# DeltaNet merges: triangular blocks joined in pairs and then in halves, as small float32 products in several column groups

## The chip, the cores and the metric

The kernel runs on one core of one Trainium2 chip. The metric is the device time of one execution in microseconds (us), lower being better. The engines of a core work side by side: TensorE (matmuls; in the profile PE, its weight loads PEld), VectorE (DVE), ScalarE (ACT), GpSimd (POOL) and SyncE (SP), which issues most DMAs.

## The reference

The network is a two-layer trunk over 512 positions with 1024 channels. Layer 0 mixes tokens by a gated DeltaNet, layer 1 by a convolution module; each layer then has a cross-attention into 256 memory positions and a squared-ReLU MLP. The change lies in the DeltaNet, whose core solves a unit lower triangular system for each head and each chunk of positions:

```python
lower = jnp.where(strict, jnp.einsum("bhnik,bhnjk->bhnij", k_beta, k) * decay, 0.0)
a_mat = jnp.eye(DN_CHUNK, dtype=q.dtype) + lower
rhs = jnp.concatenate([v * beta[..., None], k_beta * jnp.exp(g_cum)[..., None]], axis=-1)
sol = lax.linalg.triangular_solve(a_mat, rhs, left_side=True, lower=True, unit_diagonal=True)
...
def step(state, inp):
    qd, kd, uc, wc, ai, gl = inp
    v_new = uc - jnp.einsum("bhck,bhkv->bhcv", wc, state)
    o = jnp.einsum("bhck,bhkv->bhcv", qd, state) + jnp.einsum("bhcj,bhjv->bhcv", ai, v_new)
    state = state * jnp.exp(gl)[..., None, None] + jnp.einsum("bhck,bhcv->bhkv", kd, v_new)
    return state, o
```

The kernel uses chunks of 128 positions (four chunks, eight heads of 128 channels), which gives the same output, and inverts the 128x128 triangular matrix of each head and chunk instead of solving with it.

## The kernel before

**Stages and order.** `run` (in the kernel's main function) walks through a list `mains` of TensorE work, one entry being half of a projection of 128 output columns (12 matmuls with 512 moving columns, lines 292 to 294, tile `h`), or a unit of the memory's keys and values (tiles `K`, `V`). Beside each entry it issues "sides", that is, pieces of the DeltaNet with their position in the list and a rank. TensorE executes its queue in the order in which it is written, so the sides' matmuls stand between two entries' matmuls. Every large product is split into three of a faster float32 format (`wh`, `wl` are the two parts of a weight, made by ScalarE and VectorE; `xh`, `xl` those of the input); the small products of the DeltaNet are plain float32.

**The inverse.** For each head `k2` makes the matrix `bt` (128x512: four chunks side by side), a transposed triangular matrix. The four diagonal blocks of 32x32 of each matrix are inverted together for four heads on VectorE (`fs_in`, `fs_begin`, `fs_steps`, `fs_end`). The "merges" then build the 128x128 inverse from these blocks:

- `mg_pre` clears the result tile `u0` and the diagonal blocks of `bt` (on GpSimd).
- `mg_a` copies the inverted blocks onto the diagonal of `u0` and transposes it blockwise on VectorE into `x0`.
- `mg_w` (line 689) multiplies `bt` with `x0`, one product for each chunk with 128 stationary and 96 moving columns; ScalarE evicts it negated into `w` (line 691).
- `mg_y` (line 701) runs three times, the last time as `mg_end`: it multiplies `w` with the latest term `y`, with 96, 64 and 32 stationary and moving columns. ScalarE copies the next `y` (line 704), VectorE adds the product into `u0` (a helper's line, 71). The inverse is thus a sum of powers.

The recurrence over the chunks (`rec`) reads the finished tile as `U[h]`.

**Places.** Four heads (`gq` = 0 or 1) are merged together; the position is `MG[gq]` in the list, 36 and 68. Two heads take a step in the same slot, the other two one slot later, so that five slots hold the merges of a group. In the first group projections `h` stand between the slots, in the second units of `K`. PSUM tiles (`psum`, eight banks) and SBUF tiles (`slot`, 69 of them) rotate.

Of the kernel before, what the change touches and what calls it, by code (L numbers as in the profile page):

```python
# [10 lines left out]
AF = mybir.ActivationFunctionType  # L11
ALU = mybir.AluOpType
AX = mybir.AxisListType

P = 128
# [22 lines left out]
def tile_trunk(ctx, tc, xT, memT, x_d, mem_d, prm_d, adt_d, bdw_d, tap_d, fin_d, w_ab, w_kq, w_v, w_z, w_dno, w_pw1, w_pw2,  # L38
               w_q, w_k, w_vv, w_o, w_up, w_dn, yT):
    nc = tc.nc  # L40
    pe, act, dve, pool = nc.tensor, nc.scalar, nc.vector, nc.gpsimd
# [10 lines left out]
    def nm(s):  # L52
        cnt[0] += 1
        return f"{s}_{cnt[0]}"

    def slot(dt=F32, s="u", shape=(P, NT)):
        return up.tile(list(shape), dt, tag="u", name=nm(s))

    def psum(s="ps"):
        return psp.tile([P, NT], F32, tag="ps", name=nm(s))  # L60
# [9 lines left out]
    def tt(e, o, a, b, op):  # L70
        r = e.tensor_tensor(out=o, in0=a, in1=b, op=op)  # L71
        if e is pool:
            last_pool[:] = [r]
        return r
# [10 lines left out]
    def c4(t):  # L85
        return t.rearrange("p (c i) -> p c i", c=4)
# [112 lines left out]
    for kind, gq in DN_ORDER:  # L199
        for i in range(2):  # L200
            j = gq * 2 + i
# [228 lines left out]
    class DeltaNet:  # L430
# [233 lines left out]


        def mg_pre(self, h):
            u0, bt = slot(s="u0"), self.BT.pop(h)
            pool.memset(u0, 0.0)
            for b in range(4):
                bs = slice(32 * b, 32 * b + 32)  # L670
                pool.memset(c4(bt)[bs, :, bs], 0.0)
            self.M[h] = u0, bt

        def mg_a(self, h):
            (u0, bt), n = self.M[h], slice(h % 4 * 4, h % 4 * 4 + 4)
# [6 lines left out]

        def mg_w(self, h):
            u0, x0, bt = self.M[h]
            ps = psum("mg")
            for c in range(4):
                pe.matmul(c4(ps)[:, c, 0:96], bt[:, c * P:(c + 1) * P], c4(x0)[:, c, 0:96], start=True, stop=True)
            w = slot(s="w")  # L690
            self.w = act.activation(c4(w)[:, :, 0:96], c4(ps)[:, :, 0:96], AF.Copy, scale=-1.0)
            self.M[h] = u0, u0, w, 1

        def mg_y(self, h):
            u0, y, w, n = self.M[h]
            ps = psum("mg")
            r = 128 - 32 * n
            k = slice(0, 128 if n == 1 else r + 32)
            cs = slice(32 * n, 128)
            for c in range(4):  # L700
                pe.matmul(c4(ps)[0:r, c, cs], c4(w)[k, c, 0:r], c4(y)[k, c, cs], start=True, stop=True)
            if n < 3:
                y = slot(s="y")
                act.copy(c4(y)[0:r, :, 32 * n + 32:128], c4(ps)[0:r, :, 32 * n + 32:128])
            tt(dve, c4(u0)[0:r, :, cs], c4(u0)[0:r, :, cs], c4(ps)[0:r, :, cs], ALU.add)
            self.M[h] = u0, y, w, n + 1

        def mg_end(self, h):
            self.mg_y(h)
            self.U[h] = self.M.pop(h)[0]  # L710


        def ev_v(self, h):
            self.M["v", h] = self.conv_raw(self.ps.pop(("v", h)))
# [171 lines left out]
    def mem_gain(layer, half):  # L886
        gn = f"xa_mem{layer}"
        if half == 0:
            mem["xs"] = []
        for j in (2 * half, 2 * half + 1):  # L890
            if layer == 1:
                m = mem["m"][j].rearrange("p (k t) -> p k t", k=2)
                tt(dve, m, m, over_c(mem["rs"][:, 0:256], 2), ALU.mult)
            mh = slot(F32R, "mh")
            ml = slot(F32R, "ml")
            for i in range(2):
                ks = slice(i * 256, (i + 1) * 256)
                src = mem["m"][j][:, ks]
                g = pc(gn, 2 * j + i)
                act.activation(mh[:, ks], src, AF.Copy, scale=g)  # L900
                stt(ml[:, ks], src, g, mh[:, ks].bitcast(F32), ALU.mult, ALU.subtract)
                mem["xs"].append((mh[:, ks], ml[:, ks]))
# [393 lines left out]
    def taps(m):  # L1296

        TAPS[m] = []
        for i in range(9):
            t = slot(s="tap")  # L1300
            nc.sync.dma_start(out=t, in_=tap_d[m - NTAP, i])
            TAPS[m].append(t)
# [239 lines left out]
    for i in range(4):  # L1542
        s = slice(i * 256, (i + 1) * 256)
# [29 lines left out]
    D = DeltaNet(n0)  # L1573
    mains, S = [], Sides()
# [68 lines left out]
    for gq in range(2):  # L1643
        f0, nf = FS[gq]
        S.at(f0, 5, D.fs_begin, gq)
        for i in range(nf):
            S.at(f0 + i, 6, D.fs_steps, gq, i * 31 // nf, (i + 1) * 31 // nf)
        S.at(f0 + nf, 1, D.fs_end, gq)
        for h in range(4 * gq, 4 * gq + 4):
            S.at(f0 + nf, 1, D.mg_a, h)  # L1650
        S.at(f0 + 1, 7, D.norm_k, gq)
        S.at(f0 + nf + 2, 7, D.norm_q, gq)
        for i in range(4):
            h = 4 * gq + i
            S.at(f0 + nf - 4 + i, 5, D.mg_pre, h)
            for j, f in enumerate((D.mg_w, D.mg_y, D.mg_y, D.mg_end)):
                S.at(MG[gq] + j + i // 2, 1, f, h)
        for c in range(4):
            u = at["v", 4 * gq + 3] + V2[gq]
            if gq == 0:  # L1660
                S.at(u, 3, D.v2, gq, c)
            else:
                S.at(u, 3, D.v2, gq, c, (0, 1, 2))
                S.at(u + 1, 0, D.v2, gq, c, (3,))
        n = 0
        for c in range(4):
            for step in range(3):
                S.at(REC[gq] + n, 0, D.rec, gq, c, step)
                n += 1
            S.at(REC[gq] + n + (c < 3 if gq == 1 else -(c == 1)), 5, D.o_gate, gq, c)  # L1670
        S.at(ONORM[gq], 1, D.o_norm, gq)
# [33 lines left out]
    h = []  # L1705
# [13 lines left out]
    h = xattn(0, n1, h, n2)  # L1719
    n3 = Norm("cv_norm")  # L1720
    h, rest = mlp7(0, n2, h, n3, lambda: (mem_gain(1, 0), mem_gain(1, 1), taps(NTAP)))
    n4 = Norm("xa_norm1")
    h = conformer(n3, h, n4, rest)
    n5 = Norm("mlp_norm1")
    h = xattn(1, n4, h, n5)
# [30 lines left out]
MG = (36, 68)  # L1756
# [119 lines left out]
```

## Time and profile before

| | us |
|---|---|
| three runs, median | 1465.74 |
| lowest and highest | 1464.31 and 1465.99 |
| the profiled execution | 1464.05 |
| its span in the profile | 1462.3 |
| TensorE busy in the merges' products (256 matmuls) | 20.79 |

The times are those of whole executions; the profile is of one further execution, and what lies between its time and its span is 1.75 us before the first and behind the last recorded instruction. Matmuls overlap, so that "busy" of one is longer than the step to the next: the time from the start of one matmul to the start of the next is what a product costs. Tile names are those of the program without their numbers; `u` in the rows is `u0`, and the products of merges are called `mg`. A stationary operand of 96 rows and 64 columns is written `96*64`.

### The profile page before, as it was taken

What the parts mean: (1) busy time and instruction counts of PE and PEld (TensorE: products, weight loads), DVE (VectorE), ACT (ScalarE), POOL (GpSimd) and SP (SyncE); (2) the same over time, 40 slices, a digit from 0 to 9 for tenths busy, and PEclk for the clock granted to TensorE, in tenths of its full rate; (3) what the DMA queues carried; (4) which work ended last, traced back from release to release, by engine and by line L of the source; (5) the groups of instructions that cost most, each with busy time, mean ns of one, the idle gap of its engine ahead of it and who ended that gap; (6) DMA issues with size and microseconds to landing.
All of it is one profiled execution on the core that took longest, in us unless ns stands there. A gap on an engine that the chain in (4) does not pass through costs nothing.

```text
span 1462.3 us, 19656 instructions
## 1 busy us (share of the span) xinstructions
PE 1453.4 (99%) x7310; PEld 1226.7 (84%) x7310; DVE 1065.9 (73%) x1618; ACT 771.2 (53%) x1328; POOL 266.8 (18%) x289
## 2 busy tenths in 40 slices
PE   9999999999999999999999999999999999999998
PEld 7888889988888888888888889988888888888886
DVE  6879889867646766767679899985555766767677
ACT  7856865655434464435355655564444554434354
POOL 1411310103113000010000487402113000000100
PEclk9999999999999999999999999999999999999999
DMA  8232124442213666575766624533214566575853
GB/s 288 80 116 72 59 87 159 134 141 87 72 44 109 165 165 180 140 200 134 202 159 216 184 81 164 178 130 100 72 46 130 138 170 178 138 210 128 216 160 87
DMA packets 62880, 201.83 MB, mean 138 GB/s; under 512 B 7744, under 2 KB 10304, under 8 KB 62784
## 3 DMA queue, kind: packets, MB, share of 16 engines
q1 hardware_dynamic: 52560, 164.39, 33.4%
q0 software_dynamic: 9792, 35.66, 14.1%
q8 instruction: 57, 0.93, 0.3%
q10 hardware_dynamic: 432, 0.52, 0.1%
q14 instruction: 39, 0.32, 0.1%
HBM read 197.66 MB, written 2.10 MB: 137 GB/s over the span
## 4 chain that ended last, share of the span: by engine, by line
PE 93%; DVE 3%; ACT 2%; issue 1%; POOL 1%; DMA 1%; SPq 0%; DVEq 0%; POOLq 0%; ACTq 0%
PE up L294 8%; PE up L292 8%; PE up L293 8%; PE dn L1130 6%; PE dn L1128 6%; PE dn L1129 6%; PE pw L294 3%; PE pw L292 3%; PE pw L293 3%; PE h L292 2%; PE h L294 2%; PE h L293 2%; PE xo L293 2%; PE q L293 2%; PE q L292 2%; PE xo L292 2%
## 5 line engine op out<-in xcount | busy, mean ns | idle before, releaser
L251 ACT CAST wh<-raw 128x1024 fp32r<-128x1024 f32 x259 | 271.7, 1051 | 360.2 <-issue 97.0
L71 DVE TENSOR_TENSOR wl<-raw,wh 128x1024 fp32r<-128x1024 f32 (+1 forms) x250 | 304.3, 1219 | 105.7 <-ACT wh L251 99.6
L292 PE MATMUL up<-xh,wh 128*128 128x512 f32 x512 | 199.7, 390 | 0.0
L294 PE MATMUL up<-xh,wl 128*128 128x512 f32 x512 | 199.3, 389 | 0.0
L293 PE MATMUL up<-xl,wh 128*128 128x512 f32 x512 | 199.2, 389 | 0.0
L294 PEld LDWEIGHTS up<-xh,wl 128*128 128x128 f32 x512 | 96.1, 188 | 20.1
L293 PEld LDWEIGHTS up<-xl,wh 128*128 128x128 f32 x512 | 96.1, 188 | 19.9
L292 PEld LDWEIGHTS up<-xh,wh 128*128 128x128 f32 x512 | 96.1, 188 | 19.8
L239 POOL DMA_DIRECT2D t<-w_dn x48 | 42.2, 916 | 370.0 <-DVE wl L71 249.8
L1128 PE MATMUL dn<-wh,ah 128*128 128x512 f32 (+1 forms) x260 | 100.6, 387 | 0.0
L1130 PE MATMUL dn<-wl,ah 128*128 128x512 f32 (+1 forms) x260 | 100.4, 386 | 0.0
L1129 PE MATMUL dn<-wh,al 128*128 128x512 f32 (+1 forms) x260 | 100.4, 386 | 0.0
L77 DVE SCALAR_TENSOR_TENSOR rl<-up,rb 128x512 f32<-128x512 f32 x64 | 44.2, 690 | 58.3 <-PE up L294 58.3
L1388 DVE SCALAR_TENSOR_TENSOR ca<-x,prm,ca 128x512 f32<-128x512 f32 x112 | 82.3, 753 | 3.9 <-ACT ca L1385 1.5
L251 ACT CAST wh<-t 128x1024 fp32r<-128x1024 f32 x44 | 46.4, 1054 | 54.3 <-PE dn L1129 43.7
L71 DVE TENSOR_TENSOR wl<-t,wh 128x1024 fp32r<-128x1024 f32 x44 | 53.7, 1224 | 27.9 <-ACT wh L251 27.8
L292 PE MATMUL h<-xh,wh 128*128 128x512 f32 x184 | 73.7, 400 | 0.0
L71 POOL TENSOR_TENSOR sq<-sq,sq 128x512 f32<-128x512 f32 x28 | 45.4, 1620 | 148.3 <-ACT sq L385 134.2
L294 PE MATMUL h<-xh,wl 128*128 128x512 f32 x184 | 71.9, 391 | 0.0
L293 PE MATMUL h<-xl,wh 128*128 128x512 f32 x184 | 71.7, 390 | 0.0
L71 DVE TENSOR_TENSOR acc<-acc,dn 128x512 f32<-128x512 f32 x99 | 66.7, 683 | 1.2
L71 DVE TENSOR_TENSOR al<-u,ah 128x512 fp32r<-128x512 f32 x64 | 44.1, 689 | 21.4 <-ACT ah L331 21.4
(392 smaller groups left out, 3564.7 us busy)
## 6 DMA issues: line engine op xcount, KB each, us to landing
raw<-w_dn SPq DMA_DIRECT2D x68, 512.0 KB, 3.8
raw<-w_up SPq DMA_DIRECT2D x64, 512.0 KB, 4.5
t<-w_dn POOLq DMA_DIRECT2D x48, 512.0 KB, 5.8
raw<-w_pw SPq DMA_DIRECT2D x24, 512.0 KB, 3.7
raw<-w_dn POOLq DMA_DIRECT2D x20, 512.0 KB, 6.0
raw<-w_k SPq DMA_DIRECT2D x16, 512.0 KB, 3.6
raw<-w_vv SPq DMA_DIRECT2D x16, 512.0 KB, 3.9
t<-w_dn SPq DMA_DIRECT2D x16, 512.0 KB, 4.5
```

Of the source, the lines that this page charges most:

```text
L71: r = e.tensor_tensor(out=o, in0=a, in1=b, op=op)
L77: return dve.scalar_tensor_tensor(out=o, in0=a, scalar=s, in1=b, op0=op0, op1=op1)
L239: nc.gpsimd.dma_start(out=t, in_=a, accum_op=ALU.add)
L251: ins = [act.copy(h, raw)]
L292: pe.matmul(ps, wh, xh, start=first, stop=False)
L293: pe.matmul(ps, wh, xl, start=False, stop=False)
L294: pe.matmul(ps, wl, xh, start=False, stop=last)
L1128: pe.matmul(ps, xh, w[0][:, s], start=opens and k == 0, stop=False, skip_group_check=True)
L1129: pe.matmul(ps, xl, w[0][:, s], start=False, stop=False, skip_group_check=True)
L1130: pe.matmul(ps, xh, w[1][:, s], start=False, stop=k == 3, skip_group_check=True)
L1388: first["tap"] = dve.scalar_tensor_tensor(out=a, in0=src, scalar=w, in1=a, op0=ALU.mult, op1=ALU.add)
```

## The change

`mg_pre` no longer clears the diagonal blocks of `bt`. `mg_a` stays. In place of the sum of powers the blocks are joined in two rounds. In the first, `mg_w` multiplies for each chunk the two halves of `bt` (64 stationary columns each) with 32 columns of `x0`, writing to partitions 0 to 63 and 64 to 127 of one PSUM bank; `mg_y` makes from that three products of 32x32 for each chunk, written to partitions 32, 0 and 64, which fill the off-diagonal blocks of the two 64x64 halves: two in `u0`, and one, transposed, in `x0`. In the second round `mg_t` and `mg_end` make the 64x64 block that joins the halves, with 64 stationary and moving columns; `mg_half` alternates between the two heads of a pair, of which one writes to the upper and the other to the lower 64 partitions, each in its own PSUM bank. The four functions now take a pair of heads and are placed at the slots at which the pair's steps stood before.

```diff
         def mg_pre(self, h):
-            u0, bt = slot(s="u0"), self.BT.pop(h)
+            u0 = slot(s="u0")
             pool.memset(u0, 0.0)
-            for b in range(4):
-                bs = slice(32 * b, 32 * b + 32)
-                pool.memset(c4(bt)[bs, :, bs], 0.0)
-            self.M[h] = u0, bt
+            self.M[h] = u0, self.BT.pop(h)
...
-        def mg_w(self, h):
-            u0, x0, bt = self.M[h]
-            ps = psum("mg")
+        def mg_w(self, hs):
+            for h in hs:
+                u0, x0, bt = self.M[h]
+                ps = psum("mg")
+                for c in range(4):
+                    for r in (0, 64):
+                        pe.matmul(ps[r:r + 64, 32 * c:32 * c + 32], bt[:, c * P + r:c * P + r + 64], c4(x0)[:, c, r:r + 32],
+                                  start=True, stop=True)
+                w = slot(s="w")
+                self.w = act.activation(w[:, 0:P], ps[:, 0:P], AF.Copy, scale=-1.0)
+                self.M[h] = u0, x0, bt, w
+
+        def mg_y(self, hs):
+            for h in hs:
+                u0, x0, bt, w = self.M[h]
+                ps = psum("mg")
+                p3 = ps[:, 0:P].rearrange("p (c x) -> p c x", c=4)
+                for c in range(4):
+                    wc, d1, d3 = w[:, 32 * c:32 * c + 32], c4(u0)[:, c, 32:64], c4(u0)[:, c, 96:128]
+                    for r, l, m in ((32, d1, wc), (0, wc, d1), (64, wc, d3)):
+                        pe.matmul(p3[r:r + 32, c, :], l, m, start=True, stop=True)
+                act.copy(c4(x0)[32:64, :, 0:32], p3[32:64])
+                dve.tensor_copy(c4(u0)[64:96, :, 96:128], p3[64:96])
+                act.copy(c4(u0)[0:32, :, 32:64], p3[0:32])
+                self.M[h] = u0, x0, bt
+
+        def mg_half(self, hs, r0, operands, out):
+            ps = [psum("mg") for h in hs]
+            rows = [slice(abs(r0 - 64 * i), abs(r0 - 64 * i) + 64) for i in range(2)]
             for c in range(4):
-                pe.matmul(c4(ps)[:, c, 0:96], bt[:, c * P:(c + 1) * P], c4(x0)[:, c, 0:96], start=True, stop=True)
-            w = slot(s="w")
-            self.w = act.activation(c4(w)[:, :, 0:96], c4(ps)[:, :, 0:96], AF.Copy, scale=-1.0)
-            self.M[h] = u0, u0, w, 1
-
-        def mg_y(self, h):
...
-        def mg_end(self, h):
-            self.mg_y(h)
-            self.U[h] = self.M.pop(h)[0]
-
+                for h, p, r in zip(hs, ps, rows):
+                    pe.matmul(p[r, 64 * c:64 * c + 64], *operands(h, c), start=True, stop=True)
+            for h, p, r in zip(hs, ps, rows):
+                out(h, p[r, 0:256])
+
+        def mg_t(self, hs):
+            def operands(h, c):
+                u0, x0, bt = self.M[h]
+                return bt[:, c * P + 64:c * P + P], c4(x0)[:, c, 0:64]
+
+            def out(h, p):
+                t = slot(s="w")
+                act.activation(t[64:128, 0:256], p, AF.Copy, scale=-1.0)
+                self.M[h] = self.M[h][0], t
+
+            self.mg_half(hs, 64, operands, out)
+
+        def mg_end(self, hs):
+            def operands(h, c):
+                u0, t = self.M[h]
+                return t[64:128, 64 * c:64 * c + 64], c4(u0)[64:128, c, 64:128]
+
+            def out(h, p):
+                u0 = self.U[h] = self.M.pop(h)[0]
+                dve.tensor_copy(c4(u0)[0:64, :, 64:128], p.rearrange("p (c x) -> p c x", c=4))
+
+            self.mg_half(hs, 0, operands, out)
...
         for i in range(4):
             h = 4 * gq + i
             S.at(f0 + nf - 4 + i, 5, D.mg_pre, h)
-            for j, f in enumerate((D.mg_w, D.mg_y, D.mg_y, D.mg_end)):
-                S.at(MG[gq] + j + i // 2, 1, f, h)
+            for j, f in enumerate((D.mg_w, D.mg_y, D.mg_t, D.mg_end)):
+                if i % 2:
+                    S.at(MG[gq] + j + i // 2, 1, f, (h - 1, h))
```

More of the change, by code (lines that the diff above doesn't have):

```diff
@@ L681, in mg_a @@
             self.M[h] = u0, x0, bt
-        def mg_w(self, h):
-            u0, x0, bt = self.M[h]
-            ps = psum("mg")
-            for c in range(4):
-                pe.matmul(c4(ps)[:, c, 0:96], bt[:, c * P:(c + 1) * P], c4(x0)[:, c, 0:96], start=True, stop=True)
-            w = slot(s="w")
-            self.w = act.activation(c4(w)[:, :, 0:96], c4(ps)[:, :, 0:96], AF.Copy, scale=-1.0)
-            self.M[h] = u0, u0, w, 1
-        def mg_y(self, h):
[L695 to L706, printed above, removed]
```

## The prediction

> **What bounds the kernel now.** I read the page first (busy times, slices, the shares of the chain), then TensorE's waits, then the chain of work around the first group of merges, then single stretches of the timeline.
>
> ```profile
> span 1462.3 us, 19656 instructions
> PE 1453.4 (99%) x7310; PEld 1226.7 (84%) x7310; DVE 1065.9 (73%) x1618; ACT 771.2 (53%) x1328; POOL 266.8 (18%) x289
> ...
> PEclk9999999999999999999999999999999999999999
> ...
> PE 93%; DVE 3%; ACT 2%; issue 1%; POOL 1%; DMA 1%; SPq 0%; DVEq 0%; POOLq 0%; ACTq 0%
> ```
>
> TensorE is busy for the whole span at the full granted clock, and the chain that ends last runs through it. Busy time alone could hide waits, because ends of matmuls are modelled; so here are all of TensorE's recorded waits:
>
> ```profile
> engine line waited for: us in total, times, longest us
> PE warm L130 <- POOL ones L127: 1.2, 1, 1.2
> PE h L1588 <- ACT xh L378: 0.3, 1, 0.3
> PE pw L294 <- POOL wl L71: 0.2, 1, 0.2
> PE dn L1130 <- DVE wl L71: 0.2, 1, 0.2
> ```
>
> They are 1.9 us of 1462, none in the merges. The chain of waits around the first four heads' merges (columns: start, length in us, what) shows them as plain TensorE time between the projections `h`:
>
> ```profile
> 119.94 2.00 PE mg L689 x16
> 121.93 0.26 PE h L292
> ...
> 124.73 1.36 PE mg L701 x16
> 126.08 1.79 PE mg L689 x16
> 127.87 0.26 PE h L292
> ...
> 130.65 2.60 PE mg L701 x32
> 133.25 0.26 PE h L292
> ...
> 136.03 1.69 PE mg L701 x32
> 137.72 0.43 PE h L292
> ...
> 140.69 0.62 PE mg L701 x16
> 141.30 0.43 PE h L292
> ```
>
> So a microsecond that the merges take from or give back to TensorE's queue should move the end by about a microsecond. Everything else is second to the question how densely the new, smaller products can be issued. A float32 product appears here as two pairs of weight load and matmul: 8 heads times 4 chunks make 32 products of the first merge step, and its rows below count 64.
>
> **The price of one pair.** L689 (128 stationary columns): 1.79/16 = 0.112 us. L701 with 96: 1.36/16 = 0.085 us. For the smaller shapes I cut the timeline at two places, so that the difference of two rows is a count of steps in a known time:
>
> ```profile
> 130.57 0.33 PE L701 MATMUL mg<-y,w 96*64 96x64 f32 x2
> 130.57 1.03 PE L701 MATMUL mg<-y,w 96*64 96x64 f32 x14
> 264.24 0.34 PE L701 MATMUL mg<-y,w 64*32 64x32 f32 x5
> 264.24 0.63 PE L701 MATMUL mg<-y,w 64*32 64x32 f32 x14
> 44.51 0.30 PEld L531 LDWEIGHTS gsum<-g,tri_gt 128*128 128x128 f32 x2
> 44.54 0.39 PE L531 MATMUL gsum<-g,tri_gt 128*128 128x32 f32 x2
> 44.74 0.30 PEld L532 LDWEIGHTS gsum<-g,tri_le 128*128 128x128 f32 x2
> ```
>
> 64 columns: (1.03 - 0.33)/12 = 0.058 us. 32 columns: (0.63 - 0.34)/9 = 0.032 us. The last three rows say what sets the pace: 128 stationary columns with only 32 moving ones still take (44.74 - 44.51)/2 = 0.115 us a pair, as with 96 moving ones. A pair costs its stationary columns; narrowing the moving side buys nothing.
>
> **Change of the array's shape.** The slot at 140.69 holds 16 pairs of 32 columns: 0.62 + 0.43 until the projection is back in step, against 16 x 0.032 + 0.26 (the re-entry after a 128-column slot) = 0.77. Going into a narrow shape and out again costs 0.28 us. The slot at 136.03 holds 16 of 32 and 16 of 64 columns: 1.69 + 0.43 - (0.51 + 0.93 + 0.26) = 0.42, so a change between two narrow shapes costs another 0.14. The slot at 130.65: 2.60 + 0.26 - (0.93 + 1.36 + 0.26) = 0.31.
>
> **The sum, part by part.** Both versions use the same five slots a group of four heads, in the same places, so nothing moves past a projection.
>
> Before, per group: 16 pairs each of 128, 96, 64 and 32 columns, twice (two pairs of heads): 32 x (0.112 + 0.085 + 0.058 + 0.032) = 9.18 us, and shape changes of 0.31 + 0.42 + 0.28 = 1.01.
>
> After, per head: `mg_w` 8 products of 64 columns (two column groups for each chunk), `mg_y` 12 of 32 columns (three column groups), `mg_t` 4 and `mg_end` 4 of 64 columns. Per group that is 128 pairs of 64 columns and 96 pairs of 32: 224 pairs where there were 128. If they run one after another at the prices above: 128 x 0.058 + 96 x 0.032 = 10.50 us, 1.31 more than before. Every slot is now in a narrow shape: 0.28 + 0.42 + 0.42 + 0.42 + 0.28 = 1.82, 0.81 more. (`mg_end` reads 64 partitions, which I count as a shape of its own.) Two groups: +2.62 and +1.62, together +4.2 us.
>
> So by itself the arithmetic saved doesn't help: fewer multiplications, more loads. What can turn it is the placing. Neighbouring products land in different column groups (partitions 0 and 64; 32, 0 and 64; in `mg_t` and `mg_end` the one head low and the other high). No row of this trace shows that: every narrow product of before writes from partition 0. The bounds for a pair are therefore: at the top, no overlap, 0.058 and 0.032; at the bottom, loads into two groups run side by side. A product's two pairs go to the same group, so the second load has to wait for the first matmul; matmuls start in order, so at best one product's second pair coincides with the next product's first, a factor of two: 0.029 and 0.016. For the 32-column pairs something else may come first, as nothing in the rows above starts closer than 0.032; I take 0.024, the middle, for them, and 0.029 for the 64-column ones. Then 128 x 0.029 + 96 x 0.024 = 6.02 us, 3.17 less than before; two groups -6.3, with the shape changes -4.7 us. With 0.032 or 0.016 for the small ones it is -3.2 or -6.2.
>
> I take the overlapping case as the likelier, for one reason from the rows: in the stretch at 264.24 a pair takes 0.032 us although load and matmul, at 32 columns, would need about 0.028 each (a quarter of 0.112); the load is already hidden under another matmul of the same group, so loads and matmuls are separate streams in this array, and a load into cells that no other product holds has less reason to wait than one that has been seen not to wait.
>
> The Trainium skill, "TensorEngine Tiling (Array Packing)", section Tiling Modes, says that tiles are independent and that different ones can load weights and multiply in parallel. By that alone two groups would halve and three groups third the pairs, about -8 us with the shape changes, as an estimate; no run here shows it yet.
>
> **Off TensorE.** What leaves the other engines and what comes:
>
> ```profile
> L71 DVE TENSOR_TENSOR u<-u,mg x24: 268/404/544, 128.5 to 274.3; 96x384 f32<-96x384 f32 x8, 64x256 f32<-64x256 f32 x8, 32x128 f32<-32x128 f32 x8
> L704 ACT COPY y<-mg x16: 255/306/371, 127.5 to 268.2; 96x256 f32<-96x256 f32 x8, 64x128 f32<-64x128 f32 x8
> L691 ACT ACTIVATE w<-mg x8: 470/491/495, 123.5 to 255.9; 128x384 f32<-128x384 f32 x8
> L671 POOL MEMSET bt<- x32: 195/198/323, 62.1 to 196.3; 32x128 f32 x32
> ```
>
> VectorE loses 24 adds (24 x 0.404 = 9.7 us) and gets 8 copies of 32x128 (0.27 by the smallest add) and 8 of 64x256 (0.40): -4.3 us. ScalarE loses 8 x 0.49 + 16 x 0.31 = 8.8 and gets 8 + 16 pieces of 128 columns (0.26) and 8 of 256 (0.37): 9.2, no change. GpSimd loses 32 x 0.2 = 6.3 us. I cost all this at nothing: TensorE waits for none of them here. The cover is the projection's half (about 2.7 us) between two merge slots:
>
> ```profile
> 123.46 0.85 ACT L691 ACTIVATE w<-mg 128x384 f32<-128x384 f32 x2
> 124.56 1.52 PE L701 MATMUL mg<-u,w 128*96 128x96 f32 x16
> 127.47 0.62 ACT L704 COPY y<-mg 96x256 f32<-96x256 f32 x2
> 130.57 1.15 PE L701 MATMUL mg<-y,w 96*64 96x64 f32 x16
> ```
>
> `w` is ready at 124.31, 0.25 us before its reader; a third of the columns makes it earlier. `y` is ready 2.5 us early; the two copies per head in its place (the one that `mg_t` needs stands first) take perhaps 0.5 us more, which fits. Were a cover gone, TensorE would stand with the next projection queued behind it, some 0.3 us a slot, at most 3 us over ten slots. Four fewer rotating tiles a pair of heads can only free buffers earlier.
>
> **The rivals.**
>
> *Loads run one at a time.* Column groups keep the results apart but the weight path is single; the change then does not do what its placing is for. Price as above: +4.2 us, 1468.3 for the profiled execution, 1470.0 by the median: slower. With the small ones at 0.032, the two versions are even where 256 pairs of 64 columns give back the 4.2 us, 0.0166 each, so this side begins where such a pair costs more than 0.041 us. For it: the rows of `gsum`, where loads follow one another without a gap and set the pace. Against it: the reason given for the overlap. The Trainium skill, "TensorE: Matmul & The Clock Gate", section Packing small matmuls, speaks for this rival: a load overlaps running matmuls only if its row group differs, and all products of a stage here read the same rows. This trace already contradicts the sentence as it stands (0.032 us a pair in one row group), but for two loads at once it may hold. Chance 0.29.
>
> *Loads overlap, but are issued in order.* The next product's load leaves only when the matmul before it starts, which is 0.03 us after its own load (44.51 and 44.54). A 64-column product then costs 0.058 + 0.030 for two pairs, 0.044 each, and a 32-column one gains nothing: 128 x 0.044 + 96 x 0.032 = 8.70, -0.48 a group; two groups and the shape changes give +0.7 us, 1466.4: no change that can be told. Chance 0.11.
>
> *Every change of column group drains the array* like a change of shape (0.14): 8 + 12 + 4 + 4 a head, 224 in all, +31 us and the serial 4.2: about 1501. Nothing in the trace speaks for it but that the price exists. Chance 0.04. New waits on ScalarE or VectorE that outweigh a small gain: 0.04.
>
> **How the numbers follow.** The sum is made against the profiled execution, 1464.05 us (span 1462.3 and 1.75 around it); it lies 1.69 below the median of the three runs, 1465.74, so I add that. Forecast, the overlapping case with a chance of 0.52: 1464.05 - 4.7 + 1.69 = 1461.0, its own range 1459.5 to 1462.6. The range of 8 in 10 must reach the serial case: 1459.0 to 1470.5. What this kernel's measurement can tell from no change is about 0.2%, 2.9 us. Faster by more than that: nearly all of the overlapping case, 0.50. Within it: the in-order case and the rest of the first, 0.13. Slower: the serial case, the drains and new waits, 0.37.
>
> **What would show it.** In the profile after: the chain's `mg` rows give the price of a pair directly. The first `mg_w` slot of 32 pairs, its entry (0.62 - 0.51 = 0.11) included, at 1.0 us says overlap, 2.0 says one load at a time, 1.5 in order; over 4 says drains. An `mg_t` or `mg_end` slot behaves like `mg_w`; if only `mg_y` stays at 0.032, issuing is the floor there. TensorE's waits should have no new row at the merges; the rows after a slot should be 0.43 instead of 0.26 in all five slots. The forecast is wrong if the `mg` total of the chain for the first group (10.1 us in the rows above) does not fall below about 8.

## The result and the profile after

The changed kernel takes 1462.02 us (median of 12 runs, 1461.28 to 1463.06), the kernel before, run beside it, 1465.71 us (12 runs, 1464.31 to 1466.26). The ratio is 0.9977, with a 95% interval from 0.9970 to 0.9985: faster by 0.23% by this ratio, and by 3.7 us between the medians. The forecast was 1461.0. The profiled execution of the changed kernel took 1463.06 us, the longest of its twelve. First its page: span, busy times, shares of the chain that ended last.

```profile
span 1461.2 us, 19997 instructions
PE 1448.6 (99%) x7502; PEld 1220.1 (84%) x7502; DVE 1064.9 (73%) x1610; ACT 771.9 (53%) x1336; POOL 260.7 (18%) x257
...
PE 88%; DVE 7%; issue 2%; ACT 2%; POOL 1%; DMA 0%; SPq 0%; DVEq 0%; POOLq 0%; ACTq 0%
```

TensorE has 192 matmuls more and is busy for 4.8 us less. Its share of the chain fell from 93% to 88%, and VectorE's rose from 3% to 7%: something of the gain was handed to another engine. TensorE's waits, longest first, say to whom:

```profile
PE S L821 <- DVE vnd L71: 1.3, 1, 1.3
...
PE mg L713 <- ACT w L724: 0.9, 1, 0.9
PE vt L758 <- ACT cva L564: 0.7, 2, 0.5
```

Before there was none at `S` (a product of the recurrence), `mg` or `vt` (the transposes of the values). In order of time `vt` comes first, behind 145 us, then `S` at 196 us, then `mg` at 269 us, before the last `mg_end`. The other rows lie ahead of the merges or behind 300 us. Now the timeline of TensorE through the first group's merges, with the start and the length of each stretch (rows of one slot, and of the beginning and end of one run of 32-column products):

```profile
122.22 1.16 PE L688 MATMUL mg<-x,bt 128*64 128x32 f32 x32
...
130.94 0.69 PE L713 MATMUL mg<-x,bt 128*64 128x64 f32 x16
...
131.60 0.20 PE L702 MATMUL mg<-w,u 128*32 128x32 f32 x1
131.61 0.20 PE L702 MATMUL mg<-u,w 128*32 128x32 f32 x2
...
132.05 0.20 PE L702 MATMUL mg<-w,u 128*32 128x32 f32 x1
132.05 0.20 PE L702 MATMUL mg<-u,w 128*32 128x32 f32 x2
```

32 pairs of 64 columns are done in 1.16 us, so they overlap. From the row at 131.60 to the one at 132.05 lie 14 rounds of three pairs, one in each column group: 0.45/14 = 0.032 us a round, 0.0107 a pair. One round costs what one pair cost before. The trace has the starts in nanoseconds: the three pairs of a round start 7 ns apart, and two pairs of 64 columns 7 and 52 ns apart, 0.0295 us each on average.

To see where the time went, I set the start of every projection matmul (and `K`, `V`) against the start of the same matmul in the trace of before. Profiled executions differ by up to 3.5 us in the first 118 us, ahead of the first merge, with no order to it (this one lost 2.3 us there), so all such differences are counted from 118 us on:

| stretch (us of the kernel before) | changed kernel against before, us |
|---|---|
| 118 to 145, the first group's slots | -3.3 |
| 145 to 200 | +2.1 |
| 245 to 270, the second group's slots but the last | -3.5 |
| 270 to 290 | +1.35 |
| 118 to the end, all together | -3.3 |

Between 200 and 245 us and behind 290 us nothing moves. So each group gains, and each gives more than a third back right behind. Busy time by stretch shows the second half of this; the columns are the stretch, its length, busy time (and number) of PE, PEld, DVE, ACT and POOL, the granted clock, the DMA share and GB/s. First before:

```profile
118.00:146.00 28.00, 27.87 (x205) 23.34 (x205) 26.64 (x48) 20.68 (x39) 3.98 (x11) 1.00 0.17 58
146.00:160.00 14.00, 13.94 (x81) 11.78 (x80) 13.18 (x17) 10.62 (x15) 2.97 (x6) 1.00 0.20 73
255.00:272.00 17.00, 17.00 (x181) 16.38 (x180) 14.42 (x25) 11.90 (x22) 2.52 (x2) 1.00 0.21 73
```

and after:

```profile
118.00:146.00 28.00, 27.86 (x316) 22.21 (x315) 27.35 (x43) 21.89 (x44) 6.07 (x11) 1.00 0.21 69
146.00:160.00 14.00, 13.27 (x77) 11.06 (x76) 13.87 (x19) 10.09 (x14) 2.88 (x6) 1.00 0.14 44
255.00:272.00 17.00, 16.09 (x215) 15.31 (x214) 15.01 (x24) 13.21 (x29) 2.99 (x2) 1.00 0.29 103
```

VectorE was busy for 26.64 of 28 us in the first group's stage, and is now busy for 27.35 of 28 and then 13.87 of 14. The chain of waits from 121 to 152 us, by line, names the same exchange, before and then after:

```profile
by line: PE mg L701 20.2%; PE h L292 14.2%; PE h L294 11.9%; PE h L293 11.8%; issue 9.8%; PE mg L689 9.0%; DVE cva L77 5.5%; ACT cva L553 4.0%; ACT dt L539 3.7%; ACT wh L251 3.4%; ACT cva L564 3.4%; ACT dt L538 3.1%; ACT L539 0.1%
```

```profile
by line: DVE cva L77 51.8%; DVE wl L71 16.5%; issue 9.5%; DVE x L677 6.7%; DVE cv L71 4.4%; DVE u L736 4.0%; DVE u L675 3.3%; DVE u L704 3.2%; DVE L L77 2.3%; DVEq L71 0.1%
```

TensorE's lines, two thirds of this chain before, are gone from it. What sets the end of this stretch now is VectorE's queue: the taps of the convolutions (`cva`, line 77) and the low parts of the weights (`wl`), work that the change did not touch.

Followed further, the chain of before leaves TensorE right behind the first group's last slot and comes back to it only at `S`; the first row stood last in the prediction's list.

```profile
141.30 0.43 PE h L292
141.75 0.62 ACT cva L553
...
194.49 0.61 DVE vnd L71
195.10 0.04 issue
195.15 1.16 PE S L794 x8
```

Between 141.75 and 195.15 us it runs over ScalarE, VectorE, GpSimd and one transfer, though TensorE waited for none of them: the two sides reached `S` at about the same time. In the changed kernel the chain is VectorE's from 97.32 us, ahead of the merges, to 161.89 us:

```profile
96.45 0.24 PE h L294
...
97.32 0.40 DVE X L71
...
161.28 0.61 DVE vnd L71
```

So a first group that ends 3.3 us earlier on TensorE could not bring the work behind it forward by as much.

### The profile page after: what moved, and what is told of

It reads as the page before. It is cut to its first block, busy times and chain, and to the rows that moved or that the text cites. A ratio compares the mean times of both kernels' runs of the same rounds, so it can differ in the third digit from the quotient of the medians.

```text
span 1461.2 us, 19997 instructions
## 1 busy us (share of the span) xinstructions
PE 1448.6 (99%) x7502; PEld 1220.1 (84%) x7502; DVE 1064.9 (73%) x1610; ACT 771.9 (53%) x1336; POOL 260.7 (18%) x257
## 4 chain that ended last, share of the span: by engine, by line
PE 88%; DVE 7%; issue 2%; ACT 2%; POOL 1%; DMA 0%; SPq 0%; DVEq 0%; POOLq 0%; ACTq 0%
PE up L294 8%; PE up L293 8%; PE up L292 8%; PE dn L1157 6%; PE dn L1156 6%; PE dn L1155 6%; PE pw L294 3%; PE pw L292 3%; PE pw L293 3%; PE xo L293 2%; PE xo L294 2%; PE q L293 2%; PE q L292 2%; PE q L294 2%; PE xo L292 2%
```

## The experiments

All twelve ran beside the kernel before, whose median was 1464.8 to 1465.3 us there. The last two columns come from the profiled execution: the shift against before of the first group (from 118 to 245 us) and of the second (from 245 us to the end).

| kernel | median, us | ratio to before, 95% | first | second |
|---|---|---|---|---|
| changed kernel | 1462.02 | 0.9977 [0.9970, 0.9985] | -1.2 | -2.2 |
| e1, one column group | 1469.12 | 1.0026 [1.0017, 1.0036] | +2.1 | +2.2 |
| e2, group by group | 1463.94 | 0.9992 [0.9983, 1.0001] | -0.6 | -0.5 |
| e3, `mg_end` a slot later | 1460.54 | 0.9969 [0.9958, 0.9981] | -1.9 | -2.4 |
| e4, blocks on GpSimd | 1463.43 | 0.9987 [0.9978, 0.9996] | -0.7 | -0.7 |
| e5, four heads a slot | 1460.44 | 0.9968 [0.9955, 0.9980] | -0.4 | -3.6 |
| e6, e3 and taps of V | 1461.92 | 0.9978 [0.9970, 0.9987] | -0.7 | -2.3 |
| e7, e3 and `mg_a` on GpSimd | 1461.12 | 0.9972 [0.9960, 0.9983] | -1.3 | -2.3 |
| e8, e3 and V's turn later | 1461.19 | 0.9973 [0.9963, 0.9983] | -0.9 | -2.3 |
| e9, e5 and V's turn later | 1461.07 | 0.9973 [0.9964, 0.9983] | -0.9 | -3.6 |
| e10, e3 and the decay later | 1460.37 | 0.9970 [0.9959, 0.9981] | -2.3 | -2.4 |
| e11, e5 and the decay later | 1462.64 | 0.9984 [0.9975, 0.9993] | +1.2 | -3.6 |
| e12, e7 and e10 | 1461.32 | 0.9976 [0.9965, 0.9986] | -1.6 | -2.4 |

**e1: is it the column groups?** The same products in the same order, but all written from partition 0, side by side in the bank.

```diff
-pe.matmul(ps[r:r + 64, 32 * c:32 * c + 32], ...)
+pe.matmul(ps[0:64, 2 * r + 32 * c:2 * r + 32 * c + 32], ...)
...
-p3 = ps[:, 0:P].rearrange("p (c x) -> p c x", c=4)
+p3 = {r: ps[0:32, 4 * r:4 * r + P].rearrange("p (c x) -> p c x", c=4) for r in (0, 32, 64)}
...
-rows = [slice(abs(r0 - 64 * i), abs(r0 - 64 * i) + 64) for i in range(2)]
+rows = [slice(0, 64) for i in range(2)]
```

> All merge products of the changed kernel write from partition 0 (side by side in their bank), so neighbours share a column group; operands, shapes, slots and results stay, and mg_w is evicted in two pieces of 64 partitions instead of one. Theory (column groups load and multiply side by side): pairs go back to 0.058 and 0.032 us, 10.5 us a group of heads instead of some 4.7, so TensorE gets 11.5 us more work; the 4 us of waits that the changed kernel has should vanish, as TensorE is late again. Net about +7 against the changed kernel: 1469 to 1470, slower than the kernel before. Rival (the gain comes from the work taken off VectorE and GpSimd, not from the groups): no change, about 1462.

Its timeline and, for the last two rows, its chain of waits:

```profile
120.35 2.02 PE L688 MATMUL mg<-x,bt 128*64 128x32 f32 x32
125.27 0.25 PE L703 MATMUL mg<-w,u 128*32 128x32 f32 x2
125.36 0.29 PE L703 MATMUL mg<-u,w 128*32 128x32 f32 x4
...
131.83 1.15 PE L714 MATMUL mg<-x,bt 128*64 128x64 f32 x16
...
142.67 1.07 PE mg L714 x16
143.74 0.43 PE h L292
```

The first slot is back at 2.02 us, and the difference to 1.16 is 0.027 us a pair. The starts are 58 and 32 ns apart, one pair after another, and the six pairs of three products come in the order of the program: two `w,u`, then four `u,w`. In the changed kernel one `w,u` and two `u,w` alternate, so that the two pairs of a product no longer stand together. The chain's `mg` rows of this group sum to 11.6 us where before had 10.1. With the shift of +2.1 and +2.2 us a group, e1 shows the whole gain to be the column groups', and the smaller arithmetic alone to cost 4.4 us (3.8 by the medians). Nor is it the PSUM bank: in e1 the two heads of `mg_half` still write to a bank each, and 16 of their pairs take 1.15 us, where the changed kernel needs 0.69.

**e2: how far ahead does TensorE look?** The loops are exchanged, so that all four chunks of one column group come first, and in `mg_half` one head before the other.

```diff
-for c in range(4):
-    for r in (0, 64):
+for r in (0, 64):
+    for c in range(4):
...
```

> Same products in the same column groups, but in another order: all four chunks of one group first, then all of the next, and in the second round all of one head before the other. Theory that only neighbours in the queue overlap: nearly all overlap is lost, as with one group, 1468 to 1470. Rival that TensorE looks further ahead in its queue: loads of the next group are pulled past waiting ones, the time stays at 1462, or between the two by the depth it looks (0.029 and 0.011 us a pair kept, or part of it).

```profile
121.38 1.41 PE L688 MATMUL mg<-x,bt 128*64 128x32 f32 x32
...
125.71 0.34 PE L703 MATMUL mg<-w,u 128*32 128x32 f32 x5
125.86 0.22 PE L703 MATMUL mg<-u,w 128*32 128x32 f32 x1
125.89 0.20 PE L703 MATMUL mg<-w,u 128*32 128x32 f32 x1
...
131.15 0.97 PE L714 MATMUL mg<-x,bt 128*64 128x64 f32 x16
```

Between both theories: 1.41 us, where alternating groups take 1.16 and one group 2.02; for 16 pairs 0.97, where the others take 0.69 and 1.15. In `mg_y` this kernel's rows show pairs of `w,u` and `u,w` mixed at the border between two groups and alone in the middle of a group's run: the first `u,w` starts behind five of the eight `w,u` that the program has ahead of it, so not every pair starts in the order in which the queue is written. TensorE thus looks past several pairs of one group, but not past a whole run of eight; the order of the loops is worth 1.9 us of the median (2.2 by the two ratios).

**e3: the wait before `mg_end`.** What holds TensorE there is ScalarE's queue. The chain of the changed kernel, shortly before:

```profile
267.40 1.04 ACT wh L251
...
268.46 0.39 ACT w L724
...
268.89 1.07 PE mg L713 x16
```

The eviction of `mg_t` (line 724) stands behind a weight's cast (`wh`) of 1.04 us. e3 moves `mg_end` one slot later.

```diff
-S.at(MG[gq] + j + i // 2, 1, f, (h - 1, h))
+S.at(MG[gq] + j + i // 2 + (j == 3), 1, f, (h - 1, h))
```

> The changed kernel with mg_end one slot later in both groups; nothing else. In the changed kernel TensorE stands still before the last mg_end for t, which ScalarE evicts late (2.1 us later against the projections than just before). Theory (a local wait; the slot between mg_t and mg_end is too short for ScalarE's queue): the wait goes, 1460 to 1461, faster than the changed kernel by 1 to 2 us. Rival (VectorE as a whole is behind, and TensorE must wait for it somewhere): the wait comes back at the next step that needs VectorE or ScalarE, 1462.

The row `mg <- ACT w` is gone, and so is the one at `S`; the median is 1460.54, 1.5 us below the changed kernel's (1.2 by the two ratios, whose intervals overlap). The waits of the merges' surroundings in e3, the first behind the first group, the second behind the second:

```profile
PE vt L758 <- ACT cva L564: 1.4, 1, 1.4
...
PE V L325 <- DVE kf L71: 0.6, 1, 0.6
```

The wait at `vt` was 0.7 before this step, and the one at `V` is new. So the forecast time came true, but the wait was less local than the theory has it: by the table's shifts the second group, where the wait of 0.9 us went, gains only 0.2 us more, and the first group 0.7.

**e4: the blocks' eviction.** Starting from the changed kernel, the copies of `fs_in` in the second group go to GpSimd instead of VectorE (`pool.tensor_copy if gq`).

> The changed kernel with the 16 copies of diagonal blocks of the second group of heads (fs_in, 172 to 196 us, 0.27 us each on VectorE) on GpSimd, which is mostly idle there; 4.3 us less for VectorE just where TensorE waits 1.2 to 1.5 us for its vnd at 196 us. Theory (VectorE's queue gives the first group's gain back): the wait at vnd shrinks, 1460.5 to 1461.5. Rival (ScalarE's queue with its table loads sets that step): 1462; if GpSimd takes long enough to hold up the transposition of the blocks, 1462 to 1463.

```profile
PE vn L808 <- DVE r L77: 1.7, 1, 1.7
...
PE mg L688 <- DVE x L677: 1.2, 1, 1.2
PE mg L713 <- ACT w L724: 1.0, 1, 1.0
```

Worse, against the forecast. The wait at `S` goes, as the theory has it, but 1.7 us come back in the same stage, at `vn`, again for VectorE; the first merge step of the second group now waits 1.2 us for `x`, the transpose in `mg_a`; and the wait at `mg_end`, for ScalarE, stays. A copy takes 0.41 us on GpSimd, where VectorE took 0.27; whether that is what makes `x` late stays open.

**e5: four heads in one slot.** Fewer slots, so fewer changes of shape, and more time for every eviction.

```diff
-S.at(MG[gq] + j + i // 2, 1, f, (h - 1, h))
+S.at(MG[gq] + j + 1 + (j == 3), 1, f, (h - 1, h))
```

> As with mg_end later (1460.5), and the first two heads of a group now take their steps in the slots of the other two: four slots a group with four heads each (the second to the fourth of the five, and the one after the last), one narrow shape in each. Shape changes fall from six entries and two changes between narrow shapes to four entries: 2 x 0.28 + 2 x 0.14 = 0.84 us a group, 1.7 in all. Theory that TensorE sets the end there: 1458.8. Theory that VectorE (27.35 of the 28 us from 118 to 146 busy in the changed kernel) sets the first group: only the second group's 0.84 counts, 1459.7. Rival: evicting four heads at once holds up the next step on ScalarE, 1460.5 or more.

```profile
PE vt L758 <- ACT cva L564: 1.8, 1, 1.8
...
PE h L292 <- ACT u L705: 0.9, 1, 0.9
PE S L821 <- DVE vnd L71: 0.5, 1, 0.5
```

The second group gains 3.6 us, the most of all orders; the first gains 0.4: it waits 1.8 us at `vt`, where the changed kernel waits 0.7, and 0.9 at a projection inside the stage. The median of 1460.44 can't be told from e3's.

**e6 to e9: who is late at `vt`?** Four attempts, starting from e3 (e9 from e5), to save the first group's gain. e6 changes which engine takes the taps of V (`CONV_V = (1, 1, 1, 1, 1, 1, 0, 0)`). e7 moves the first group's copies in `mg_a` from VectorE to GpSimd (`dve.tensor_copy if h > 3 else pool.tensor_copy`). e8 puts V's turn one entry later (`V2 = (11, 9)`), e9 does so in e5.

> As with mg_end later, and one tap of the value convolution of heads 2 and 3 goes from VectorE (0.74 us each) to ScalarE and GpSimd. If VectorE's queue gives back the first group's gain (1.4 us of waiting for the last value head's taps at vt), 1.5 us less of it brings 1 to 1.5: 1459.0 to 1459.5. Rival, ScalarE's queue is as late: 1460.5.

> As with mg_end later, and the eight copies by which mg_a puts the first group's inverted blocks on the diagonal (VectorE, some 0.28 us each, 118 to 123 us) go to GpSimd, 0.4 us each by the copies of blocks measured there. VectorE gets 2.3 us earlier through the merges. If it sets the pace there: 1458.5 to 1459.5. Rival: the copies are ahead of the first merge step, so slower ones make TensorE wait for x0: 1460.5 to 1462.

> As with mg_end later (1460.5), and the transposes of the first group's values (v2, tile vt) one slot later, two slots ahead of the recurrence that reads them. There TensorE waits 1.4 us for ScalarE's silu of the last tap. If that wait is as local as the one before mg_end, it goes: 1459.1 to 1459.5, and the recurrence still has what it needs. Rival, VectorE and ScalarE are the bound of the whole stretch from 118 to 200 us: the wait comes back at the recurrence (vn, S), 1460.5.

> The same step on the kernel with four heads a slot (1460.4, with 1.8 us of waiting at vt). Local wait: 1458.6 to 1459.2. Bound of the whole stretch: 1460.4.

None is faster than the kernel it starts from, and e6 is 1.4 us slower than e3. The row `vt <- ACT cva` reads 2.4, 1.5, 1.5 and 2.2 us in them. e7 shows best that it isn't VectorE's sum of work alone (its stretch, then its waits):

```profile
118.00:146.00 28.00, 28.00 (x320) 22.19 (x319) 24.68 (x36) 23.21 (x47) 8.86 (x20) 1.00 0.20 64
...
PE vt L758 <- ACT cva L564: 1.5, 1, 1.5
...
PE S L821 <- DVE vnd L71: 1.1, 1, 1.1
```

VectorE has 3.3 us to spare in the stage, and TensorE waits as long as in e3, and once more at `S`.

**e10 to e12: ScalarE's order.** The `cva` for which `vt` waits stands on ScalarE behind the decay's activations of heads 4 and 5. e10 puts the decay one entry later in e3 (`DEC1 = (40, 45)`), e11 in e5, and e12 joins e10 and e7.

> As with mg_end later (1460.5), and the decay of heads 4 and 5 one slot later, behind the silu of the last value head instead of ahead of it. On ScalarE that decay is two relus, two exps and two loads of function tables of 1.28 us, about 5 us in all, and TensorE waits 1.4 us at vt for the silu behind them. If ScalarE's order sets that wait, it goes: 1459.0 to 1459.5. Rival, VectorE's last taps set it: 1460.5.

> The same on the kernel with four heads a slot (1460.4, 1.8 us of waiting at vt): 1458.6 to 1459.2 if ScalarE's order sets the wait, 1460.4 if VectorE's taps do.

> mg_end a slot later, with both reliefs of the stage from 118 to 160 us at once: the first group's copies of mg_a that were VectorE's on GpSimd, and the decay's activations one slot later. Alone, the first left TensorE's wait at vt for ScalarE at 1.5 us, the second took that wait away and left 0.6 at vt for VectorE. Theory that the first group's gain is given back to both queues together, each behind the other: TensorE's waits from 140 to 200 us fall below 0.8 in sum, about 1 us less from 118 us to the end, ratio to before 0.9963 (1459.6 us). Rival, that what arrives earlier is held by something that neither relief touches (the transfers or the order of the slots): waits of some 1.5 us in that stage again under other names, ratio 0.997 (1460.4 us).

The waits behind the first group, e10's, then e12's:

```profile
PE vt L758 <- DVE u L736: 0.6, 1, 0.6
PE S L821 <- DVE vnd L71: 0.4, 1, 0.4
```

```profile
PE vt L758 <- DVE u L736: 0.9, 2, 0.6
...
PE vt L758 <- ACT cva L564: 0.5, 1, 0.5
PE S L821 <- DVE vnd L71: 0.4, 1, 0.4
```

e10 removes the wait for ScalarE, and smaller ones for VectorE come up in its place: the same median as e3, as the rival has it. ScalarE now stands idle for 3.36 us ahead of the same `cva`, until VectorE has done its tap. In e12 VectorE and ScalarE are both relieved and the two still share 1.8 us between them, near the rival's 1.5 and not below the theory's 0.8; its median, 1461.32, lies above both forecasts. e11 is slower and misses both of its own: its profiled execution loses 5 us between 145 and 180 us, of which waits at `vt` are 2.4; the cause stays open. So the first group's gain is given back in part between 145 and 200 us in every order that was tried, to VectorE and ScalarE by turns: at most 2.3 us of it arrive (e10). Which chain of their work sets that limit is not settled: no run took work from both without putting it elsewhere in the same stage. The best versions, e3, e5 and e10, lie 1.5 to 1.7 us below the changed kernel's median (1.0 to 1.3 by the ratios), and can't be told from one another.

## Why the prediction was right

The time came out 1.0 us above the forecast, on its side and for its main reason, but two terms of the sum were wrong in opposite directions: the small pairs gave 2.4 us more than forecast, and 3.8 us that were put at nothing were lost. That the number came so close is in part luck.

*TensorE bounds the kernel:* right for before in that TensorE's waits were 1.9 us. The step drawn from it, that a microsecond off TensorE's queue moves the end by about a microsecond, holds inside the merges' stages and fails behind them: the first group gained 3.3 us in its slots and 1.2 in the end. The trace of before had both warnings. VectorE was busy for 26.64 of the 28 us of the first group's stage, and the chain left TensorE one row behind the last one that the prediction shows. The prediction drew on neither.

*Serial prices and shape changes:* right. The sum +4.2 us forecast for loads one after another is what e1 measures: +4.4. The sign announced for the shapes, 0.43 in the row after each of the five slots, is what e1's chain shows. The rival "loads run one at a time", 0.29, was thus priced well and is false.

*The 64-column pair at 0.029:* right (0.0295).

*The 32-column pair at 0.024:* the mis-sized term; it is 0.0107, below even the lower end of 0.016. The step that failed is the argument "matmuls start in order, so at best one product's second pair coincides with the next product's first, a factor of two". The pairs of different groups do not start in the order of the products, so the second pair of one product needn't hold up the next, and three groups give a factor of three. The other reason for 0.024, that nothing starts closer than 0.032, was a limit within one group: between groups starts lie 7 ns apart. By the right prices a group costs 128 x 0.0295 + 96 x 0.0107 = 4.80 us instead of 9.18; two groups -8.8, with the shape changes of 1.62 about -7.1, where -4.7 was forecast. The slots bear this out: -3.3 and -3.5 us, together -6.8. The Trainium skill, "TensorEngine Tiling (Array Packing)", section Tiling Modes, whose independent tiles the prediction put at about -8 us, agrees with this trace: two groups halve and three groups third the pair. The -8 was summed wrongly: by the prediction's own prices, halved and thirded, it is -7.3. The Trainium skill, "TensorE: Matmul & The Clock Gate", section Packing small matmuls, agrees in part: its table has a speedup for three column tiles, but its rules let a load overlap only with another row group, and have matmuls start strictly in order; here all pairs of `mg_w` read the same 128 rows and go at half the price in two column groups, the pairs of `mg_y` alternate between products, and in e2 pairs of a later product start ahead of earlier products' pairs.

*"I cost all this at nothing":* the other failed step. The evictions themselves were sized well: ScalarE's 64x256 takes 0.378 us against 0.37 forecast, VectorE's 0.422 against 0.40. But the cover of 2.7 us between two slots was counted as if the evicting engine were free when the product ends. In the second group a cast of 1.04 us stands ahead (with a slot more in e3 the wait is gone), and in the first the engines behind the merges were nearly full. What is missing between the prices, -7.1, and the shift, -3.3, is 3.8 us; TensorE's wait rows at `S`, `mg` and `vt` account for 2.9 of it, and the cause of the rest stays open. The prediction had this as a rival of 0.04 and "at most 3 us"; the price was near, its chance far too low.

*The signs:* the first slot near 1.0 us came as announced (1.16 with the last matmul's tail); that the five slots fall below 8 us holds too (their rows cover 6.6). The sign that TensorE's waits have no new row at the merges was false, and that was the sign to look at.

## What to carry to other kernels

In this kernel small float32 products cost their weight loads; written to different column groups of the array, with the groups alternating in the program, a pair costs half with two groups and a third with three; without that, splitting a product into smaller ones made the kernel slower. When a bound engine is relieved by some us in a stage, look up first how much slack the next engine has in that very stage, and follow the chain of waits past the stage: here VectorE had 1.4 us of 28, against 3.6 us freed by the prices. An eviction counts as covered only if nothing long stands ahead of it on its engine.

## What the hardware showed unexpectedly

Pairs of load and matmul in three column groups start 7 ns apart, where pairs of one group need 32 ns at the same size. TensorE takes pairs of other groups ahead of the second pair of a product, and in e2 ahead of three more pairs of earlier products, but only from near by: with the groups one after the other instead of alternating, 32 pairs took 1.41 us, between 1.16 and 2.02.
